# Spatial projection: the features' parts are stored in the first half and fetched in the second, with ten seven-product pairs there instead of six

## The chip, the core and the metric

The kernel runs on one core of a Trainium2 chip. The metric is the device time of one execution in microseconds. Before the change three executions took 2465.49, 2465.73 and 2466.3 us; the median is 2465.73.

## What is computed

A trunk of two layers on 256 positions of width 2048, all in float32. The first layer is a gated MLP with a spatial gate, then a gated MLP with a convolution; the second is latent attention, then the same kind of MLP. After each of the four comes a layer norm. What the change touches is the last product of the first part:

```
z = gelu(x @ w_in);  u, v = split(z, 2);  v = layer_norm(v)
s = einsum('gij,bnjgd->bnigd', masked w_s, v) + b_s
m = (u * s) @ w_out          # (256 x 6144) @ (6144 x 2048): the spatial projection
x = layer_norm(ALPHA * x + m)
```

`u * s` is called the features here.

## The kernel before

**Three products for one.** A float32 operand is split into a high part (a cast to float32r on ACT, ScalarE) and a low part (the value less its high part, a subtraction on DVE, VectorE). A product is made of three matmuls on PE (TensorE): high by high, low by high, high by low (`prod_b`). Weights are split as they are loaded (`Feed._split`, `_cast`, lines 125 and 128): `wh`, `wl`. Features are split in `Acts.make` (lines 487 and 488).

**Units, wide and seven.** The 6144 features are 48 blocks of 128, two blocks to a unit: units 0 to 23. The 2048 output columns are done in two halves of 1024, and each half goes over all 24 units, so each unit is used twice: 0 to 23 in the first half, 23 to 0 in the second. For a unit and a half there are 2 row blocks (positions) x 2 column blocks of 512 x 2 feature blocks, eight products. A **wide** unit (`e` in `PLAN`) makes all eight (`Banks.eight`): 24 matmuls of 512 columns. A **seven** (`s`) makes seven products of sums of blocks instead (`Banks.seven`): 21 matmuls. For that DVE adds up weight blocks (`ts`, line 135), and their sums are split as well (`th`, `tl`), so that such a unit takes five buffers of weights instead of two; and four sums of feature blocks are made (`turn`, lines 291 to 294) and split (lines 483 and 484). The seven-product sums of a half are put together once, after its last seven (`rest`, lines 450 to 454, and `fold`).

**Order and buffers.** `PLAN` is written by hand: for each half the units in order with their kinds. `down` goes through it: for each unit it calls `acts.make` for this unit and the two behind it, takes weights from the feed (split two to three units ahead), and issues the matmuls. Features made in the first half are dropped from `acts.got` and made again in the second half, but for those that are used again very soon (`KEEP`). Loaded weights have three buffers (`raw`), loads go through SP's queue. Split weights and split features share one pool of 14 buffers of 1 MB (`big`). A wide unit's features take half a buffer; two wide units share one, and it is free when both have been used (`self.room`). A seven's features take a buffer. An instruction that writes a buffer waits until the last matmul that reads its former content is done. The last three units of the second half, 2, 1 and 0, are held back (`skew`) and multiplied at the end, one output bank after the other, so that the layer norm can begin on the first bank.

Names in the profile: `wo_q`, `wo_p`, `wo_e` are the output banks of the second half; `wo8sx` is the split features of unit 8 made as a seven, `wo8st` its sums, `wo7wx` a buffer of wide units whose first is 7; `ub` the banks of the first half; `raw` loaded weights; `res` the residual; `lnt` the transposes of the layer norm that follows.

**Stores and fetches that are there already.** In the two later down projections some pairs are "parked": split ahead of time, stored in DRAM through POOL's queue (`kept...`) and fetched through the same queue (`fwh`, `fwl`, `fth`, `ftl`), four transfers of 768 KB to 1 MB one behind the other.

Of the kernel before, what the change touches and what calls it, by code (L numbers as in the profile page):

```python
# [21 lines left out]
NF_GM = HALF // P  # L22
# [32 lines left out]
T1, T2 = 6, 5  # L55
# [4 lines left out]


PLAN = {NF_GM: ("0e 1e 2s 3e 4e 5s 6e 7e 8s 9e 10e 11s 12e 13e 14s 15e 16e 17s 18e 19e 20s 21e 22e 23e",
                "23e 22e 21e 20s 19e 18e 17s 16e 15e 14s 13e 12e 11s 10e 9e 8s 7e 6e 5s 4e 3e 2e 1e 0e"),
        NF_FF: ("0e 1p 2e 3s 4e 5e 6p 7e 8s 9e 10e 11p 12e 13s 14e 15p 16e 17s 18e 19s 20e 21e",
                "21e 20e 19p 18e 17s 16e 15p 14e 13s 12e 11p 10s 9e 8s 7p 6e 5s 4e 3e 2e 1e 0e")}
KINDS = {"e": "wide", "s": "seven", "p": "parked"}
# [143 lines left out]
def trunk(ctx: ExitStack, tc: tile.TileContext, x, xT, gm_in, gm_wout, ffn_up, ffn_dn,  # L210
          ml_q, ml_kv, ml_b, ml_out, consts, w_sT, b_s, ropes, ln_rows, out):
    nc = tc.nc
# [25 lines left out]
    def behind(ins):  # L238

        if recent[0] is not None and feed.used > 0:  # L240
            order(ins, recent[0])
# [46 lines left out]
    def turn(t, k1, k2):  # L288

        at = lambda k, b: k[:, b] if len(k.shape) == 3 else k[:, b * P : (b + 1) * P]  # L290
        tc.keep_in_program_order(nc.vector.tensor_tensor(t[:, 0], at(k1, 0), at(k1, 1), ALU.subtract))
        nc.vector.tensor_tensor(t[:, 1], at(k1, 1), at(k2, 1), ALU.subtract)
        nc.vector.tensor_tensor(t[:, 2], t[:, 1], at(k1, 0), ALU.subtract)
        nc.vector.tensor_tensor(t[:, 3], at(k2, 0), t[:, 2], ALU.add)
# [11 lines left out]
    for j in range(4):  # L306
        t = slot([P, 4, S], f"xraw{j}", tag="side")
# [97 lines left out]
    class Banks:  # L405


        def __init__(self, tag, names, tiles=None):
            self.tag, self.begun = tag, set()
            self.acc = dict(zip(names, tiles)) if tiles else {n: bank(f"{tag}_{n}") for n in names}  # L410
# [45 lines left out]

    class Acts:

        def __init__(self, src, tag, n_k):
            self.src, self.tag, self.n_k = src, tag, n_k  # L460
            self.got, self.room = {}, None

        def make(self, u, kind, tag="big"):

            if u in self.got and (kind == "wide" or self.got[u][1]):
                return
            name, n = f"{self.tag}{u}{kind[0]}", min(2, self.n_k - 2 * u)
            x = self.src[u // 4][:, 2 * u % 8 : 2 * u % 8 + n]
            if kind == "wide":
                if self.room is None:  # L470
                    self.room = slot([P, 4, 512], f"{name}x", F32R, tag)
                    t = self.room[:, 0:n]
                else:
                    t, self.room = self.room[:, 2 : 2 + n], None
                hi, lo = t[:, :, 0:S], t[:, :, S : 2 * S]
                sums = None
            else:
                r = slot([P, 2, 8 * P], f"{name}x", F32R, tag)
                flat = [r[:, h].rearrange("p (s c) -> p s c", s=8) for h in range(2)]
                hi, lo = [r[:, h, 0 : 4 * P].rearrange("p (k c) -> p k c", k=2) for h in range(2)]  # L480
                t = tp.tile([P, 4, P], F32, tag="t2", name=f"{name}t", bufs=T2)
                turn(t, x[:, 0], x[:, 1])
                nc.scalar.copy(flat[0][:, 4:8], t)
                tc.keep_in_program_order(nc.vector.tensor_tensor(flat[1][:, 4:8], t, flat[0][:, 4:8].bitcast(F32), ALU.subtract))
                sums = [(flat[0][:, 4 + i], flat[1][:, 4 + i]) for i in (1, 2, 0, 3)]
            by = (lambda t: t.rearrange("p n (b c) -> p n b c", b=2)) if len(x.shape) == 4 else lambda t: t
            nc.scalar.copy(by(hi), x)
            tc.keep_in_program_order(nc.vector.tensor_tensor(by(lo), x, by(hi).bitcast(F32), ALU.subtract))
            parts = [[(hi[:, j, b * P : (b + 1) * P], lo[:, j, b * P : (b + 1) * P]) for j in range(n)]
                     for b in range(2)]  # L490
            self.got[u] = (parts, sums)
# [108 lines left out]
    class Norm:  # L600
# [150 lines left out]
    for gi in range(6):  # L751
# [3 lines left out]
        for c, p in enumerate(V_PAIRS[gi]):  # L755
# [29 lines left out]
        for i, (n, t) in enumerate(zip(DIRECT, rest)):  # L785
            o = vt[:, i // 2, (i % 2) * 512 : (i % 2) * 512 + 512]
# [48 lines left out]
        norm_v(0, f, rows)  # L835

    pT = [t.rearrange("p b (f c) -> p f b c", c=P) for t in v]
    acts = Acts(pT, "wo", NF_GM)
    def spatial(g, tiles):

        for i, t in enumerate(tiles):
# [25 lines left out]
    for g in range(6):  # L867
# [26 lines left out]
        for i, t in enumerate(rest):  # L894
            o = v[g][:, i // 2, i % 2 * 512 : i % 2 * 512 + 512]
# [133 lines left out]
    for c in range(6):  # L1029
        hi, lo = feed.next()  # L1030
# [321 lines left out]
```

## Time and profile before

| what | value |
|---|---|
| median of three timed executions | 2465.73 us |
| span of the profiled execution | 2464.6 us |
| PE busy | 2458.1 us, 12494 matmuls |
| DVE busy | 2054.7 us |
| ACT busy | 1459.3 us |
| POOL busy | 104.2 us |
| spatial projection, second half, first to last of its banks' regular units | 662.4 to 772.8 us |
| moved by DMA | 611.94 MB, 248 GB/s on average |

The profile is of one execution, taken apart from the timed ones; the span runs from its first to its last instruction, and no time of that execution other than the span is given. Timeline rows hold the start in us, the duration in us, the engine and line, the operation and its tiles, how many follow each other, and in brackets the idle time before and what ended it. Durations overlap the next instruction by a little, so costs are read from start to start. Matmuls overlap too: a pair of 0.61 us and one of 0.39 are 0.68 us from start to start.

### The profile page before, as it was taken

The numbers are of one execution on the slowest core, as the hardware profiler recorded it, in microseconds if no ns is written. First come the engines' busy times: TensorE is split into PE (matmuls) and PEld (weight loads), VectorE is DVE, ScalarE is ACT, GpSimd is POOL, SyncE is SP. The second block draws the span as 40 slices with busy tenths as digits, with TensorE's granted clock in tenths as the row PEclk, the third lists the DMA queues.
The fourth block names the chain that finished last, engine by engine and source line by source line (L and its number), as shares of the span: only waits on it lengthen the run. The fifth ranks groups of instructions, "written<-read, shape, count | busy, mean of one in ns | idle before, by whom it ended". The sixth has DMA issues, their size and how long they took to land. (4 is left out here: it accounts for less than half of the span.)

```text
span 2464.6 us, 32483 instructions
## 1 busy us (share of the span) xinstructions
PE 2458.1 (100%) x12494; PEld 2091.3 (85%) x12494; DVE 2054.7 (83%) x2734; ACT 1459.3 (59%) x1967; POOL 104.2 (4%) x202
## 2 busy tenths in 40 slices
PE   9999999999999999999999999999999999999999
PEld 7888888888888888888888888988888888888887
DVE  7999999989897788778777997867598787878798
ACT  6666665566565666656554566665565665555453
POOL 0000000000000000000001000000000000000000
PEclk9999999999999999999999999999999999999999
DMA  7555666656665778778868885544478787777885
GB/s 291 202 208 205 226 204 202 205 188 205 222 212 198 241 282 314 300 279 300 322 218 318 301 301 182 184 170 156 172 269 309 275 305 304 295 265 278 299 324 201
DMA packets 116428, 611.94 MB, mean 248 GB/s; under 512 B 10648, under 2 KB 10912, under 8 KB 75184
## 3 DMA queue, kind: packets, MB, share of 16 engines
q1 hardware_dynamic: 90128, 462.47, 52.9%
q0 software_dynamic: 26144, 147.39, 15.8%
q8 instruction: 98, 1.61, 0.3%
q14 instruction: 58, 0.48, 0.1%
HBM read 544.75 MB, written 65.06 MB: 247 GB/s over the span
## 5 line engine op out<-in xcount | busy, mean ns | idle before, releaser
L128 DVE TENSOR_TENSOR wl<-raw,wh 128x1024 fp32r<-128x1024 f32 (+4 forms) x645 | 958.4, 1501 | 169.5 <-ACT wh L125 124.0
L125 ACT CAST wh<-raw 128x1024 fp32r<-128x1024 f32 (+4 forms) x645 | 809.0, 1278 | 356.8 <-PE up L230 80.7
L230 PE MATMUL up<-xhl,wh 128*128 128x512 f32 x2624 | 611.4, 390 | 0.0
L230 PEld LDWEIGHTS up<-xhl,wh 128*128 128x128 f32 x2624 | 487.4, 188 | 97.8
L230 PEld LDWEIGHTS up<-xhl,wl 128*128 128x128 f32 x2624 | 325.8, 192 | 6.4
L230 PE MATMUL up<-xhl,wl 128*128 128x256 f32 x2624 | 328.1, 283 | 0.0
L125 ACT CAST th<-ts 128x1536 fp32r<-128x1536 f32 (+1 forms) x138 | 142.5, 1052 | 110.9 <-DVE ts L135 80.3
L230 PE MATMUL ub<-wh,xhl 128*128 128x512 f32 x576 | 179.5, 393 | 0.0
L128 DVE TENSOR_TENSOR tl<-ts,th 128x1536 fp32r<-128x1536 f32 (+1 forms) x138 | 163.2, 1221 | 10.4 <-PE dn_p L230 3.4
L230 PEld LDWEIGHTS ub<-wh,xhl 128*128 128x128 f32 x576 | 108.1, 188 | 24.2 <-issue 1.9
L230 PE MATMUL ub<-wl,xhl 128*128 128x512 f32 x288 | 112.1, 389 | 0.0
L135 DVE TENSOR_TENSOR ts<-ts,raw 128x512 f32<-128x512 f32 x138 | 95.1, 689 | 1.4
L135 DVE TENSOR_TENSOR ts<-raw 128x1024 f32<-128x1024 f32 x69 | 84.3, 1221 | 6.1 <-PE ub L230 3.8
L230 PE MATMUL mo<-wh,oT 128*128 128x512 f32 x256 | 82.5, 401 | 0.0
L230 PE MATMUL v_q<-wh,xhl 128*128 128x512 f32 x224 | 70.7, 391 | 0.3 <-ACT wh L125 0.3
L230 PEld LDWEIGHTS ub<-wl,xhl 128*128 128x128 f32 x288 | 54.1, 188 | 11.3
L230 PE MATMUL v_p<-wh,xhl 128*128 128x512 f32 x192 | 59.9, 389 | 0.0
L230 PEld LDWEIGHTS mo<-wh,oT 128*128 128x128 f32 x256 | 45.5, 189 | 7.1
L230 PEld LDWEIGHTS v_q<-wh,xhl 128*128 128x128 f32 x224 | 42.0, 188 | 10.5 <-ACT wh L125 1.9
L230 PE MATMUL mo<-wl,oT 128*128 128x512 f32 x128 | 50.1, 391 | 0.0
L724 ACT ACTIVATE lny<-lnt,lncol 128x128 f32<-128x128 f32 x96 | 36.6, 472 | 15.6 <-PE lnt L720 15.5
L388 DVE TENSOR_TENSOR h_0a<-up,lo_0a 128x256 f32<-128x256 f32 x41 | 17.2, 421 | 33.0 <-ACT lo_0a L386 33.0
(1838 smaller groups left out, 4338.4 us busy)
## 6 DMA issues: line engine op xcount, KB each, us to landing
raw<-in_ffn_up_dram SPq DMA_DIRECT2D x172, 1024.0 KB, 7.0
raw<-in_gm_in_dram SPq DMA_DIRECT2D x93, 1024.0 KB, 5.3
raw<-in_ffn_dn_dram SPq DMA_DIRECT2D x68, 1024.0 KB, 7.2
raw<-in_gm_wout_dram SPq DMA_DIRECT2D x48, 1024.0 KB, 5.3
praw<-in_ffn_dn_dram POOLq DMA_DIRECT2D x16, 1024.0 KB, 13.9
keptth<-pth POOLq DMA_DIRECT2D x16, 1024.0 KB, 8.1
kepttl<-ptl POOLq DMA_DIRECT2D x16, 1024.0 KB, 8.8
fth<-keptth POOLq DMA_DIRECT2D x16, 1024.0 KB, 9.4
```

The source lines that it names most:

```text
L125: cast = self.nc.scalar.copy(hi, raw)
L128: self.nc.vector.tensor_tensor(lo, raw, hi.bitcast(F32), ALU.subtract)
L135: add = lambda o, a, b: self.nc.vector.tensor_tensor(o, a, b, ALU.add)
L230: recent[0] = nc.tensor.matmul(o, l, r, start=start, stop=stop, skip_group_check=True)
L388: nc.vector.tensor_tensor(h, acc[:, 0:S], lo, ALU.add)
L724: nc.scalar.activation(y[:, j], t[:, j * P : (j + 1) * P], AF.Identity, bias=lncol[:, o : o + 1], scale=lncol[:, g : g + 1])
```

## The change

In the first half each unit from 3 to 21 has its split features stored in DRAM right after they are made (`keep`). In the second half `make` looks whether a unit was stored. If it was stored in the kind now wanted, the whole buffer is fetched and nothing is computed. If it was stored wide and is wanted as a seven (16, 13, 10 and 7), its high and low parts are fetched in two transfers and only the sums are made and split. Units 23, 22, 2, 1 and 0 are as before. In the second half's line of `PLAN` four more units become sevens: 16, 13, 10 and 7. Stores and fetches all go through POOL's queue.

```diff
-                "23e 22e 21e 20s 19e 18e 17s 16e 15e 14s 13e 12e 11s 10e 9e 8s 7e 6e 5s 4e 3e 2e 1e 0e"),
+                "23e 22e 21e 20s 19e 18e 17s 16s 15e 14s 13s 12e 11s 10s 9e 8s 7s 6e 5s 4e 3e 2e 1e 0e"),
...
+        def keep(self, u, kind, t):
+
+            if u not in self.store or u in self.away:
+                return
+            d = dram.tile(list(t.shape), F32R, tag=f"{self.tag}{u}away", name=f"{self.tag}{u}away", bufs=1)
+            tc.keep_in_program_order(nc.gpsimd.dma_start(d, t))
+            self.away[u] = (kind, d)
+
+        def fetch(self, o, d):
+
+            ins = tc.keep_in_program_order(nc.gpsimd.dma_start(o, d))
+            behind(ins)
...
+            was, d = self.away.get(u, (None, None))
...
+                if was == kind:
+                    self.fetch(t, d)
...
+                if was == kind:
+                    self.fetch(r, d)
+                else:
+                    if was:
+                        for o, c in ((hi, slice(0, S)), (lo, slice(S, 2 * S))):
+                            self.fetch(o, d[:, :, c])
+                    t = tp.tile([P, 4, P], F32, tag="t2", name=f"{name}t", bufs=T2)
+                    turn(t, x[:, 0], x[:, 1])
+                    nc.scalar.copy(flat[0][:, 4:8], t)
...
-            nc.scalar.copy(by(hi), x)
-            tc.keep_in_program_order(nc.vector.tensor_tensor(by(lo), x, by(hi).bitcast(F32), ALU.subtract))
+            if was is None:
+                nc.scalar.copy(by(hi), x)
+                tc.keep_in_program_order(nc.vector.tensor_tensor(by(lo), x, by(hi).bitcast(F32), ALU.subtract))
+                self.keep(u, kind, t if kind == "wide" else r)
...
-    acts = Acts(pT, "wo", NF_GM)
+    acts = Acts(pT, "wo", NF_GM, [u for u in range(3, 22)])
```

How this moves the instructions is seen at three places of the second half. The first is DVE, from the end of unit 14's weights on. Before, with unit 13 wide: `wo13wx` are the parts of its features and of unit 12's, the two rows `wl` of 2048 columns the weights of 13 and 12, `wo11st` and `wo8st` sums of features, `ts_5283` unit 11.

```order
L128 TENSOR_TENSOR tl_5175<-ts_5171,th_5174 128x1536
L128 TENSOR_TENSOR tl_5175<-ts_5171,th_5174 128x512
L488 TENSOR_TENSOR wo13wx<-v_1373,wo13wx 128x2x256
L128 TENSOR_TENSOR wl_5215<-raw_5138,wh_5214 128x2048
L488 TENSOR_TENSOR wo13wx<-v_1373,wo13wx 128x2x256
L128 TENSOR_TENSOR wl_5247<-raw_5185,wh_5246 128x2048
L291 TENSOR_TENSOR wo11st<-v_1070 128x128
L292 TENSOR_TENSOR wo8st<-v_1070 128x128
L293 TENSOR_TENSOR wo8st<-wo8st,v_1070 128x128
L294 TENSOR_TENSOR wo8st<-v_1070,wo8st 128x128
L135 TENSOR_TENSOR ts_5283<-raw_5218 128x1024
L484 TENSOR_TENSOR wo11sx<-wo11st,wo11sx 128x512
```

The same stretch of DVE after the change, with unit 13 a seven (`ts_5246`, `wl_5248`, `tl_5250`), down to unit 12's weights (`wl_5288`):

```order
L128 TENSOR_TENSOR tl_5203<-ts_5199,th_5202 128x1536
L128 TENSOR_TENSOR tl_5203<-ts_5199,th_5202 128x512
L291 TENSOR_TENSOR wo13st<-v_1373 128x128
L135 TENSOR_TENSOR ts_5246<-raw_5174 128x1024
L292 TENSOR_TENSOR wo10st<-v_1070 128x128
L135 TENSOR_TENSOR ts_5246<-ts_5246,raw_5174 128x512
L128 TENSOR_TENSOR wl_5248<-raw_5174,wh_5247 128x1536
L507 TENSOR_TENSOR wo13sx<-wo13st,wo13sx 128x512
L135 TENSOR_TENSOR ts_5246<-ts_5246,raw_5174 128x512
L128 TENSOR_TENSOR tl_5250<-ts_5246,th_5249 128x1536
L128 TENSOR_TENSOR tl_5250<-ts_5246,th_5249 128x512
L128 TENSOR_TENSOR wl_5288<-raw_5213,wh_5287 128x2048
```

Where one subtraction of 2048 columns stood for unit 13 stand six steps and the split of its sums; the two feature parts of 13 and 12 are gone, and so is unit 11's split of its own sums and features.

The second place is POOL's queue. Before, the last rows of the gate's normalization (`vr`) are followed by the next stage's parked pairs:

```order
L808 DMA vr_3433<-gbrows 128x512
L808 DMA vr_3506<-gbrows 128x512
L808 DMA vr_3508<-gbrows 128x512
L162 DMA praw_6409<-in_ffn_dn_dram 128x2x1024
L629 DMA resd_0_6940<-res_0_4608 128x2048
```

After, 19 stores and then 23 fetches stand between them; these are the last stores and the fetches down to unit 13 (`x2`: high and low part apart):

```order
L469 DMA wo20away<-wo20sx 128x2048
L469 DMA wo21away<-wo21wx 128x1024
L474 DMA wo23wx<-wo21away 128x1024
L474 DMA wo20sx<-wo20away 128x2048
L474 DMA wo19wx<-wo19away 128x1024
L474 DMA wo19wx<-wo18away 128x1024
L474 DMA wo17sx<-wo17away 128x2048
L474 DMA wo16sx<-wo16away 128x2x256 x2
L474 DMA wo15wx<-wo15away 128x1024
L474 DMA wo14sx<-wo14away 128x2048
L474 DMA wo13sx<-wo13away 128x2x256 x2
L474 DMA wo15wx<-wo12away 128x1024
```

The wide units of a shared buffer are now 21 with 23, 19 with 18, 15 with 12, 9 with 6, and 4 with 3; the store of each unit is ahead of every fetch in the queue.

The third place is the end of the half on DVE, from the weights of unit 2 (`wl_5590` before, `wl_5629` after) to the features of unit 0. Before:

```order
L128 TENSOR_TENSOR wl_5586<-raw_5524,wh_5585 128x2048
L128 TENSOR_TENSOR wl_5590<-raw_5557,wh_5589 128x2048
L658 SCALAR_TENSOR_TENSOR res_1_5507<-res_1_5507,wo1p_5618 128x512
L451 TENSOR_TENSOR wo1u_5619<-wo_p_4900,wo1p_5618 128x512
L452 TENSOR_TENSOR wo1w<-wo_q_4898,wo1u_5619 128x512
```

After:

```order
L128 TENSOR_TENSOR wl_5625<-raw_5568,wh_5624 128x2048
L683 SCALAR_TENSOR_TENSOR res_1_5551<-res_1_5551,wo1p_5657 128x512
L451 TENSOR_TENSOR wo1u_5658<-wo_p_4938,wo1p_5657 128x512
L128 TENSOR_TENSOR wl_5629<-raw_5597,wh_5628 128x2048
L452 TENSOR_TENSOR wo1w<-wo_q_4936,wo1u_5658 128x512
```

Unit 2's weights have moved behind the first two steps that fold the seven-product sums; all steps of the end are still there.

More of the change, by code (lines that the diff above doesn't have):

```diff
@@ L457, in trunk, with __init__ @@
     class Acts:
-        def __init__(self, src, tag, n_k):
+        def __init__(self, src, tag, n_k, store=()):
             self.src, self.tag, self.n_k = src, tag, n_k
             self.got, self.room = {}, None
+            self.store, self.away = store, {}
+        def keep(self, u, kind, t):
[7 more added lines that the diff above has]
+            behind(ins)
         def make(self, u, kind, tag="big"):
@@ L480, in make @@
                 hi, lo = [r[:, h, 0 : 4 * P].rearrange("p (k c) -> p k c", k=2) for h in range(2)]
[L481 to L484, printed above, removed]
+                if was == kind:
[7 more added lines that the diff above has]
+                    nc.scalar.copy(flat[0][:, 4:8], t)
+                    tc.keep_in_program_order(nc.vector.tensor_tensor(flat[1][:, 4:8], t, flat[0][:, 4:8].bitcast(F32), ALU.subtract))
                 sums = [(flat[0][:, 4 + i], flat[1][:, 4 + i]) for i in (1, 2, 0, 3)]
             by = (lambda t: t.rearrange("p n (b c) -> p n b c", b=2)) if len(x.shape) == 4 else lambda t: t
-            nc.scalar.copy(by(hi), x)
-            tc.keep_in_program_order(nc.vector.tensor_tensor(by(lo), x, by(hi).bitcast(F32), ALU.subtract))
+            if was is None:
+                nc.scalar.copy(by(hi), x)
+                tc.keep_in_program_order(nc.vector.tensor_tensor(by(lo), x, by(hi).bitcast(F32), ALU.subtract))
+                self.keep(u, kind, t if kind == "wide" else r)
             parts = [[(hi[:, j, b * P : (b + 1) * P], lo[:, j, b * P : (b + 1) * P]) for j in range(n)]
```

## The prediction

> **What bounds the kernel now.** I read the table of engines first, then the list of what TensorE (PE) waited for, then the stage that the change touches, stretch by stretch.
>
> ```profile
> PE 2458.1 (100%) x12494; PEld 2091.3 (85%) x12494; DVE 2054.7 (83%) x2734; ACT 1459.3 (59%) x1967; POOL 104.2 (4%) x202
> ```
>
> ```profile
> PE warm L230 <- POOL idle L281: 1.3, 1, 1.3
> PE fin L230 <- DVE dg L701: 0.3, 1, 0.3
> PE v_q L230 <- ACT wh L125: 0.3, 1, 0.3
> ```
>
> The first row is the page's, the other three are the whole answer on PE's waits. They are every wait of PE that the trace names: 1.9 us in all, at the start, in the first projection and at the very end. None lies in the spatial projection. So in this stage time is won only by giving PE fewer matmuls, and lost only by making PE wait where it doesn't now.
>
> The stretches below hold five times three units of the second half, 17 to 3, of 15.64 us each; the sum row is over all five. The columns are PE, weight loads, DVE (VectorE), ACT, POOL, granted clock, DMA share and GB/s.
>
> ```profile
> 694.57:710.21 15.64, 15.64 (x71) 12.95 (x70) 15.04 (x20) 9.40 (x9) 0.00 (x0) 1.00 0.66 233
> ...
> sum 78.20, PE 78.20 PEld 64.75 DVE 69.61 ACT 47.51 POOL 0.00; mean PE 15.64 PEld 12.95 DVE 13.92 ACT 9.50 POOL 0.00
> ```
>
> PE is full at clock 1.00. DVE has 69.6 of 78.2 us: it is the engine that can become late. ACT has a third to spare.
>
> **The matmuls removed.** From the timeline of PE, the first matmul of unit 8 (a seven), of unit 7 (wide), of the unit after, and of unit 0 among the held-back ones:
>
> ```profile
> 741.49 0.61 PE L230 MATMUL wo_q<-wh,wo8sx 128*128 128x512 f32 x2
> ...
> 746.25 0.61 PE L230 MATMUL wo_q<-wh,wo7wx 128*128 128x512 f32 x2
> ...
> 751.69 0.61 PE L230 MATMUL wo_q<-wh,wo7wx 128*128 128x512 f32 x2
> ...
> 775.49 0.61 PE L230 MATMUL wo_q<-wh,wo0wx 128*128 128x512 f32 x2
> ```
>
> (The row at 751.69 still says wo7wx because units 7 and 6 share a buffer.) A seven takes 746.25 - 741.49 = 4.76 us for 21 matmuls, a wide unit 751.69 - 746.25 = 5.44 us for 24: 0.227 us each either way. Units 16, 13, 10 and 7 become sevens: 4 x 0.68 = **2.72 us** less on PE, on the path that sets the end. That is the most the change can give, since no PE wait is there to be removed. It is 0.11%; a measurement of this kernel can tell about 0.2%, 4.9 us, from no change.
>
> **What DVE gets instead.** The timeline of DVE through one round of the half: the four small sums of a seven's features, the pair sums ts, the feature parts, the weight parts wl and tl.
>
> ```profile
> 724.58 0.29 DVE L291 TENSOR_TENSOR wo8st<-v 128x128 f32<-128x128 f32 x1
> ...
> 726.05 1.23 DVE L135 TENSOR_TENSOR ts<-raw 128x1024 f32<-128x1024 f32 x1 [0.33 <-PE wo_q L230]
> 727.19 0.68 DVE L484 TENSOR_TENSOR wo8sx<-wo8st,wo8sx 128x512 fp32r<-128x512 f32 x1
> 727.79 0.68 DVE L488 TENSOR_TENSOR wo8sx<-v,wo8sx 128x512 fp32r<-128x512 f32 x1
> 728.39 0.68 DVE L135 TENSOR_TENSOR ts<-ts,raw 128x512 f32<-128x512 f32 x1
> 729.00 1.75 DVE L128 TENSOR_TENSOR wl<-raw,wh 128x1536 fp32r<-128x1536 f32 x1
> 730.66 0.68 DVE L135 TENSOR_TENSOR ts<-ts,raw 128x512 f32<-128x512 f32 x1
> 731.27 2.35 DVE L128 TENSOR_TENSOR tl<-ts,th 128x1536 fp32r<-128x1536 f32 x2
> 733.54 0.68 DVE L488 TENSOR_TENSOR wo7wx<-v,wo7wx 128x512 fp32r<-128x512 f32 x1
> 734.14 2.28 DVE L128 TENSOR_TENSOR wl<-raw,wh 128x2048 fp32r<-128x2048 f32 x1
> 736.34 0.68 DVE L488 TENSOR_TENSOR wo7wx<-v,wo7wx 128x512 fp32r<-128x512 f32 x1
> ```
>
> Start to start, a seven's weights cost 1.14 + 0.61 + 1.66 + 0.61 + 2.27 = 6.29 us, a wide unit's 2.20, a feature part 0.60, four small sums 726.05 - 0.33 - 724.58 = 1.14. Per round of three units: before, one seven, two wide, four feature parts, four sums: 6.29 + 4.40 + 2.40 + 1.14 = 14.2 us against 15.64 of PE. After, two sevens, one wide, and for the unit that was stored wide the sums and one part: 12.58 + 2.20 + 1.14 + 0.60 = **16.5 us against 14.96**. So in the four rounds 16-5 DVE falls back 1.5 us a round; the parts not remade (9 wide units, 6 sevens, the wide part of four more) don't make up for four more sevens. DVE must live on its lead, and the lead is capped by the 14 buffers of the pool.
>
> In the built order, the last weight part of unit 16 (tl) takes a buffer that unit 18's last matmul frees, so it can't start before PE reaches unit 17, at 694.57 in this trace. From there DVE has to do, up to the low part of unit 0: that tl 2.27, seven more sevens 44.0, nine wide units 19.8, sums and part of 13, 10 and 7 5.2, the eight steps that fold the seven-product sums, and three feature parts 1.8. The fold and the end of the line, with the two idles left after the last seven:
>
> ```profile
> 752.13 2.29 DVE L128 TENSOR_TENSOR wl<-raw,wh 128x2048 fp32r<-128x2048 f32 x1 [1.38 <-ACT wh L125]
> ...
> 757.16 4.49 DVE L128 TENSOR_TENSOR wl<-raw,wh 128x2048 fp32r<-128x2048 f32 x2 [2.13 <-issue]
> 761.57 0.69 DVE L658 SCALAR_TENSOR_TENSOR res<-res,wo1p 128x512 f32<-128x512 f32 x1
> ...
> 766.50 0.68 DVE L488 TENSOR_TENSOR wo2wx<-v,wo2wx 128x512 fp32r<-128x512 f32 x1
> ...
> 772.11 0.68 DVE L488 TENSOR_TENSOR wo0wx<-v,wo0wx 128x512 fp32r<-128x512 f32 x1
> ```
>
> The fold is 766.50 - 761.57 = 4.9 us. Sum 78.0: DVE ends this at 694.57 + 78.0 = 772.6 if it never idles. PE wants it at 775.49 - 2.72 = 772.8. Today it is ready at 772.79 for a use at 775.49, with 2.7 us of cover; afterwards the cover is 0.2 us, and each idle of DVE goes straight to PE at unit 0. Bounds: no idle, a stall of 0; both idles above remain (3.5 us), 3.3. The 2.13 came from buffers that PE freed, and PE now comes earlier while DVE comes later, so I take 1.0 us of idle: a stall of **0.8 us**. Ahead of it the cover never goes below zero by the same sums; it is thinnest at unit 7, whose tl ends about 1.5 us before its first use.
>
> **The transfers.** Stored: 13 wide units of 512 KB and 6 sevens of 1 MB, 12.5 MB; fetched: 9 x 0.5 + 6 x 1 + 4 x 0.5 MB, the same. All go through POOL's queue, which in this stage has nothing else; behind them stands the first load of the next stage's parked pairs, which is made only in the up projection. The nearest rows are weight loads and the later stages' stores and fetches (KB each, median us to landing):
>
> ```profile
> raw<-in_ffn_dn_dram SPq DMA_DIRECT2D x68, 1024.0 KB, 7.2
> raw<-in_gm_wout_dram SPq DMA_DIRECT2D x48, 1024.0 KB, 5.3
> ...
> keptth<-pth POOLq DMA_DIRECT2D x16, 1024.0 KB, 8.1
> ...
> ftl<-kepttl POOLq DMA_DIRECT2D x16, 1024.0 KB, 11.9
> ```
>
> For fth, the issue on POOL in ns and the spread of landing:
>
> ```profile
> L187 POOL DMA_DIRECT2D fth<-keptth x16: 528/531/563, 1207.4 to 2394.8; - x16
> ...
> DMA to landing us min/median/max: 7.2/9.4/21.4
> ```
>
> For fwh, 768 KB and first of its four in the queue, between 1300 and 1385 us:
>
> ```profile
> DMA to landing us min/median/max: 5.7/7.0/9.4
> ```
>
> A 1 MB fetch for a seven takes a buffer that is free after nine matmuls of the seven three units ahead: 2.72 + 4.76 + 5.44 = 12.9 us of room. fth, 9.4, fits; ftl's 11.9 has 2.5 MB before it in its queue, which a fetch here hasn't. The fetches of 15 and 9 wait for the last matmul of 18 and 12 and have two sevens, 9.5 us, 4's has 10.2: at 512 KB, by fwh's 7.0 for 768 KB, they fit with 2.5 us left. Cost 0. The weight loads get slower, 5.3 to about 7.2 us, but one is issued as soon as the weights three units back are read, and DVE then has at least 2.27 + 6.29 + 2.20 = 10.8 us of other work: 0. In the first half only stores are added: a part is written two units (4.76 + 5.44 = 10.2 us) or more before PE has read it and its buffer can be taken again, against 8.1 for a 1 MB store: 0.
>
> A round now moves three weight loads and 2 MB of features, 5 x 1.05 = 5.24 million bytes in 14.96 us: 350 GB/s, where the first round above has 233. The mean rates in 40 slices of the span, and what the chip carried in a later stage while PE was full:
>
> ```profile
> GB/s 291 202 208 205 226 204 202 205 188 205 222 212 198 241 282 314 300 279 300 322 218 318 301 301 182 184 170 156 172 269 309 275 305 304 295 265 278 299 324 201
> ```
>
> ```profile
> 1310.00:1320.00 10.00, 10.00 (x46) 8.26 (x44) 6.39 (x9) 5.31 (x6) 0.00 (x0) 1.00 1.06 418
> 1320.00:1330.00 10.00, 10.00 (x46) 8.28 (x45) 9.20 (x13) 4.38 (x5) 0.00 (x0) 1.00 0.69 255
> 1330.00:1340.00 10.00, 10.00 (x46) 8.29 (x45) 3.99 (x4) 4.43 (x6) 2.11 (x4) 1.00 0.97 342
> 1340.00:1350.00 10.00, 10.00 (x46) 8.29 (x45) 9.93 (x16) 5.10 (x6) 0.00 (x0) 1.00 1.03 403
> ```
>
> The mean of the four is 354 with bursts to 418, and no wait of PE. So 350 is carried, with a sixth to spare. [...]
>
> **Sum.** -2.72 + 0.8 = -1.9 us. The profiled execution spans 2464.6 us, 1.1 under the median of the three timed runs, 2465.73; the saving is the same in both. Forecast **2463.8 us**, its own range 2463.0 to 2465.2.
>
> **Rivals.**
> The tail eats the gain. DVE keeps idles of 3 us or more after the last seven and unit 0 is late by the whole 2.7: **2465.7**. For it: the two idles above, and 78.2 - 69.6 = 8.6 us in which DVE isn't busy in the five rounds; against: an idle that ends on a buffer from PE shrinks when DVE's lead does.
> Late fetches, the slower side. The features of 15, 9 and 4 come after PE is there. This decides from 9.5 us of landing. At ftl's 11.9 PE waits 2.4 + 2.4 + 1.7 = 6.5 us, DVE catches up meanwhile, and the time is 2465.7 - 2.7 + 6.5 = **2469.5**; it passes the 0.2% at 12.3 us, or by one fetch at fth's 21.4. For it: 350 GB/s over 60 us, where no slice above has over 324. Against: fwh never took over 9.4 in the stretch shown, and these are smaller.
> POOL held up by DVE. If a descriptor write on POOL had to wait for the running DVE instruction, each fetch would land up to 2.3 us later (the longest step), 9.3 for fwh's 7.0 and 11.7 for fth's 9.4: just in time. With two such waits in a fetch, 11.6 and 14.0: 2.1 + 2.1 + 1.4 us at 15, 9 and 4, and 1.1 at each of the sevens 14, 11, 8 and 5, 10 us together: **2473**. Against: fth's issue took 528 to 563 ns in all 16 cases. [...]
> That the change doesn't do what it says: "not remade" is not quite so, since 16, 13, 10 and 7 remake their sums; this is in the sum above.
>
> **Chances.** Forecast 0.69; tail 0.14; late fetches 0.14, half of it over 4.9 us; POOL 0.02; something faster that no row shows 0.01. Faster by over 0.2%: 0.01; within: 0.69 + 0.14 + 0.07 = 0.90; slower: 0.07 + 0.02 = 0.09. The range goes from the full gain less the 0.4 us by which the runs differ, 2462.6, to 2467.6, which takes in the tail and the first part of the late fetches.
>
> **What would show it.** PE 12 matmuls fewer; the first normalization transposes 1.5 to 2.7 us earlier than now; PE's waits naming DVE wo0wx with 0.3 to 1.5 us; DVE's waits in units 16 to 5 nearly gone; fetches of 512 KB at 6 to 7.5 us, 1 MB at 8 to 10; some 350 GB/s from 695 to 755 us. Waits of PE on a fetch, or on wl or tl of units 13 to 5, would prove the working wrong.

## The result and the profile after

The changed kernel takes 2470.92 us (median of 14 runs, 2468.97 to 2472.63); the kernel before, run beside it, 2465.61 us (14 runs, 2464.89 to 2466.3). The ratio is 1.0022 with a 95% interval of 1.0014 to 1.0029: 5.3 us slower. The forecast was 2463.8 us, in a range up to 2467.6. The profiled execution of the changed kernel spans 2469.1 us, that of before 2464.6.

The table of engines of the changed kernel. PE has its 12 matmuls less:

```profile
PE 2457.8 (100%) x12482; PEld 2090.9 (85%) x12482; DVE 2055.4 (83%) x2725; ACT 1454.8 (59%) x1954; POOL 127.9 (5%) x244
```

All of PE's waits in the changed kernel (who waited for whom: us in total, times, longest). Three of the rows are new, and all three lie in the last units of the half:

```profile
PE wo_q L230 <- DVE wo2wx L512: 3.7, 1, 3.7
PE warm L230 <- POOL idle L281: 1.3, 1, 1.3
PE wo_q L230 <- DVE wo0wx L512: 0.7, 1, 0.7
PE fin L230 <- DVE dg L726: 0.3, 1, 0.3
PE wo_q L230 <- DVE wl L128: 0.2, 1, 0.2
```

The timeline of PE in the changed kernel: first matmul of unit 2 (the first of the held-back units), the next one, first of unit 0, the next one, and the first transposes of the layer norm behind the half:

```profile
770.47 0.39 PE L230 MATMUL wo_q<-wh,wo2wx 128*128 128x512 f32 x1
774.60 0.56 PE L230 MATMUL wo_q<-wh,wo2wx 128*128 128x512 f32 x1 [3.74 <-DVE wo2wx L512]
...
779.08 0.39 PE L230 MATMUL wo_q<-wh,wo0wx 128*128 128x512 f32 x1
780.21 0.50 PE L230 MATMUL wo_q<-wh,wo0wx 128*128 128x512 f32 x1 [0.74 <-DVE wo0wx L512]
...
790.14 0.60 PE L745 MATMUL lnt<-ident,res 128*128 128x128 f32 x4
```

The same two points in the kernel before:

```profile
772.77 0.61 PE L230 MATMUL wo_q<-wh,wo2wx 128*128 128x512 f32 x2
...
785.24 0.60 PE L720 MATMUL lnt<-ident,res 128*128 128x128 f32 x4
```

Up to unit 2 the change does what it should: PE is there at 770.47, 2.30 us sooner than before. Then all of it is lost and more: the transposes come 4.90 us later than before. From 770.47 to 774.60 one matmul of 0.23 us was made, so 3.90 us are lost; from 779.08 to 780.21 another 0.90. Between these two, 11 matmuls take 779.08 - 774.60 = 4.48 us where 11 x 0.227 = 2.50 would do: 1.98 us. The windows of the changed kernel show PE's clock there, and the stages before it (columns as in the prediction; the clock is the first of the last three):

```profile
700.00:720.00 20.00, 20.00 (x90) 16.58 (x89) 19.97 (x24) 11.98 (x11) 3.90 (x6) 1.00 0.96 341
720.00:740.00 20.00, 20.00 (x90) 16.57 (x89) 19.93 (x23) 11.87 (x11) 3.03 (x5) 1.00 1.00 334
740.00:755.00 15.00, 15.00 (x68) 12.40 (x67) 14.49 (x14) 9.23 (x7) 2.31 (x4) 1.00 0.97 338
755.00:765.00 10.00, 10.00 (x45) 8.07 (x43) 4.05 (x2) 2.39 (x2) 0.00 (x0) 1.00 1.02 404
...
774.00:776.00 2.00, 1.40 (x4) 1.14 (x5) 2.00 (x2) 1.15 (x2) 0.00 (x0) 0.73 0.25 102
776.00:778.00 2.00, 1.89 (x6) 0.98 (x4) 2.00 (x3) 1.24 (x2) 0.00 (x0) 0.50 0.27 33
```

After the wait the granted clock is 0.73, then 0.50. The sum is -2.30 + 3.90 + 1.98 + 0.90 = +4.5 of the 4.9 us at the transposes; 0.4 us is spread behind them. The 1.98 us are only where PE lost the time: the second matmul of unit 0 starts at 780.21 us because DVE is done with `wo0wx` at 779.47 + 0.69 = 780.16 (row below), so at full clock PE would have waited there instead.

The upper rows tell where it began. From 700 us on the DMA share is 0.96 to 1.02: the DMA engines are full. And from 755 to 765 us, while they move 404 GB/s, DVE works 4.05 us of 10. It waits for ACT, and ACT for weights. ACT in the changed kernel, the casts of the weights of units 4, 3 and 2:

```profile
752.78 1.91 ACT L125 CAST wh<-raw 128x2048 fp32r<-128x2048 f32 x1
761.02 1.91 ACT L125 CAST wh<-raw 128x2048 fp32r<-128x2048 f32 x1 [6.33 <-DMA raw<-in_gm_wout_dram]
...
766.11 1.91 ACT L125 CAST wh<-raw 128x2048 fp32r<-128x2048 f32 x1 [2.70 <-DMA raw<-in_gm_wout_dram]
```

DVE in the changed kernel, the low parts of the same three, the rest of the fold of the sevens (it begins at 765.17 and goes on at 770.26), and the first and the last low part of the features that PE waits for:

```profile
754.73 2.29 DVE L128 TENSOR_TENSOR wl<-raw,wh 128x2048 fp32r<-128x2048 f32 x1 [0.24 <-ACT wh L125]
762.96 2.29 DVE L128 TENSOR_TENSOR wl<-raw,wh 128x2048 fp32r<-128x2048 f32 x1 [5.95 <-ACT wh L125]
...
768.05 2.29 DVE L128 TENSOR_TENSOR wl<-raw,wh 128x2048 fp32r<-128x2048 f32 x1 [1.59 <-ACT wh L125]
770.26 0.68 DVE L452 TENSOR_TENSOR wo1w<-wo_q,wo1u 128x512 f32<-128x512 f32 x1
...
773.86 0.69 DVE L512 TENSOR_TENSOR wo2wx<-v,wo2wx 128x512 fp32r<-128x512 f32 x1
...
779.47 0.69 DVE L512 TENSOR_TENSOR wo0wx<-v,wo0wx 128x512 fp32r<-128x512 f32 x1
```

In these rows the low weights of 2 (768.05) stand ahead of the rest of the fold (770.26), and the fold ahead of `wo2wx` (773.86); so when the weights of unit 2 land late, everything behind them is late by as much. From 768.05 us to the end of `wo0wx` DVE has no idle time left in which it could catch up. The load of unit 2, in the changed kernel (the answer on `raw` for the stretch around 752 us) and in the kernel before (around 748 us):

```profile
L96 SPq DMA_DIRECT2D raw<-in_gm_wout_dram x1: 379/379/379, 752.3 to 752.3; - x1
...
DMA to landing us min/median/max: 13.7/13.7/13.7
```

```profile
L96 SPq DMA_DIRECT2D raw<-in_gm_wout_dram x1: 378/378/378, 747.6 to 747.6; - x1
...
DMA to landing us min/median/max: 5.5/5.5/5.5
```

It is issued 4.7 us later and takes 8.2 us longer: the weights of 2 land at 766.0 instead of 753.1 us. The issue is late because it waits for DVE to be done with the buffer, the weights three units back (DVE's last sum of them ends at 751.54 + 0.68 = 752.22 us, the issue comes at 752.3), and DVE is behind with four more sevens. What is under way beside it, from SP's and POOL's timelines of the changed kernel: the residual's second half, the loads of 3 to 0, the fetch of 3, and the first load of the next stage's parked pairs.

```profile
744.08 0.81 SPq L644 DMA_DIRECT2D res<-in_x_dram  x2
748.11 17.54 SPq L96 DMA_DIRECT2D raw<-in_gm_wout_dram  x4
```

```profile
749.62 0.54 POOL L474 DMA_DIRECT2D wo4wx<-wo3away  x1
750.14 0.73 POOL L162 DMA_DIRECT2D praw<-in_ffn_dn_dram  x1
```

That last load stood elsewhere before. POOL in the kernel before:

```profile
668.59 0.72 POOL L162 DMA_DIRECT2D praw<-in_ffn_dn_dram  x1 [222.85 <-DVE wo20sx L488]
```

It was made as soon as a buffer was free, at 668.6 us, where the DMA share is 0.57 in the 20 us around it. Now the stores and fetches of 19 units stand ahead of it on POOL, the last of them at 749.62 us, and it goes at 750.14, into the fullest stretch.

### The profile page after: what moved, and what is told of

Read it like the earlier page. It is cut to its first block, busy times and chain, and to the rows that moved or that the text cites. A ratio compares the mean times of both kernels' runs of the same rounds, so it can differ in the third digit from the quotient of the medians.

```text
span 2469.1 us, 32569 instructions
## 1 busy us (share of the span) xinstructions
PE 2457.8 (100%) x12482; PEld 2090.9 (85%) x12482; DVE 2055.4 (83%) x2725; ACT 1454.8 (59%) x1954; POOL 127.9 (5%) x244
## 5 line engine op out<-in xcount | busy, mean ns | idle before, releaser
L125 ACT CAST th<-ts 128x1536 fp32r<-128x1536 f32 (+1 forms) x146 | 150.9, 1051 | 128.9 <-DVE ts L135 104.0
L128 DVE TENSOR_TENSOR tl<-ts,th 128x1536 fp32r<-128x1536 f32 (+1 forms) x146 | 172.7, 1222 | 11.4 <-ACT th L125 3.4
L135 DVE TENSOR_TENSOR ts<-ts,raw 128x512 f32<-128x512 f32 x146 | 100.7, 690 | 1.5
```

What stands on the lines that cost most here:

```text
L125: cast = self.nc.scalar.copy(hi, raw)
L128: self.nc.vector.tensor_tensor(lo, raw, hi.bitcast(F32), ALU.subtract)
L135: add = lambda o, a, b: self.nc.vector.tensor_tensor(o, a, b, ALU.add)
```

## The experiments

The theory after this reading (theory 1): the weights of 3 and 2 land late because of the transfers that are moved at the end of the half; PE then runs into DVE's chain. Its rival (theory 2): ten sevens are too much for DVE, so the tail is late whatever the transfers do. A third: all the added traffic slows everything a little. The runs of before beside these kernels had medians of 2465.6 to 2465.9 us. A table at the end of this section sets the kernels side by side.

**Each half of the change alone.** The changed kernel with the six sevens of before:

```diff
-   "23e 22e 21e 20s 19e 18e 17s 16s 15e 14s 13s 12e 11s 10s 9e 8s 7s 6e 5s 4e 3e 2e 1e 0e"),
+   "23e 22e 21e 20s 19e 18e 17s 16e 15e 14s 13e 12e 11s 10e 9e 8s 7e 6e 5s 4e 3e 2e 1e 0e"),
```

> The changed kernel with the six sevens of before: features stored and fetched, no matmul saved. Theory 1 (a burst of transfers at the end of the half delays the weight load of unit 3, so that DVE gets the weights of 2 and 0 late): the burst is the same, so PE still waits 2 to 4 us at units 2 and 0; before is 2465.6, so 2467.5 to 2470. Theory 2 (four more sevens are too much for DVE at the tail, whatever the transfers do): DVE has less work than before, so no wait at the tail, 2465.6 within 0.5. Theory 3 (the sum of all the added traffic slows everything a little): 2466 to 2468, with small waits outside the tail.

2466.14 us, ratio 1.0003 (0.9994 to 1.0012): no difference. Theory 1's 2467.5 to 2470 is missed; the time lies at the edges of what theories 2 and 3 gave. But its trace shows slow loads all the same: unit 2's takes 12.8 us, and ACT waits 4.9 us for it. PE doesn't wait at the tail, for two reasons. With six sevens DVE is less behind, so this load is issued at 747.0 us instead of 752.3 and its weights land at 759.8 instead of 766.0. And PE comes to unit 2 1.8 us later, at 772.25. So the traffic alone takes away the cover and costs nothing yet.

And the ten sevens with nothing stored:

```diff
-    acts = Acts(pT, "wo", NF_GM, [u for u in range(3, 22)])
+    acts = Acts(pT, "wo", NF_GM)
```

> The changed kernel with nothing stored: ten sevens, all features remade. A round of three units costs DVE 12.58 + 2.20 + five feature parts 3.0 + two times four sums 2.28 = 20.1 us against 14.96 of PE, 5.1 us too much in each of four rounds, less a lead of some 8 to 12 us. All theories expect waits of PE on weights in units 13 to 5 and at the tail: 2471 to 2478. If it came out at 2463 to 2465 the transfers alone would be the loss and the sevens would need no fetches.

2479.17 us (5 runs), ratio 1.0055 (1.0042 to 1.0068), a little over what was expected. Two of PE's waits in this kernel, on weights that ACT doesn't get done; they lie in the sevens of units 10 and 7:

```profile
PE wo_q L230 <- ACT wh L125: 2.3, 2, 2.0
PE wo_q L230 <- ACT th L125: 2.0, 2, 1.0
```

The four more sevens need the fetches: those are worth 2479.2 - 2470.9 = 8.3 us to them.

**The first parked load moved out of the way.** First ahead, between the fetches of 19 and 18:

```diff
+                if hf == 1 and i == 2 and tag == "wo":
+                    feed.load_early(parked[0])
...
-        raw = tile("praw", F32)
-        pin(nc.gpsimd.dma_start(raw.rearrange("p (k c) -> p k c", k=ap.shape[1]), ap))
+        raw = self.early.pop(i, None)
+        if raw is None:
+            raw = tile("praw", F32)
+            pin(nc.gpsimd.dma_start(raw.rearrange("p (k c) -> p k c", k=ap.shape[1]), ap))
```

> The changed kernel, but the first parked pair's load (praw, 1 MB) stands in POOL's queue behind the fetch of unit 19 instead of behind that of unit 3, so it goes at about 670 to 690 us as before. Theory 1 with praw as the last straw of the burst: unit 3's weights land in time, the waits at 2 and 0 fall from 4.4 to under 1.5 us, PE's clock there stays at 1.00: 2463.5 to 2466. Theory 2 (DVE): as the changed kernel, 2470.9 within 0.7. Theory 3 (all the traffic): half of the loss at most goes, 2468.5 to 2470.5.

Then behind, through SP's queue in its place of the up projection:

```diff
-        pin(nc.gpsimd.dma_start(raw.rearrange("p (k c) -> p k c", k=ap.shape[1]), ap))
+        load = nc.sync if len(self.kept) == 1 else nc.gpsimd
+        pin(load.dma_start(raw.rearrange("p (k c) -> p k c", k=ap.shape[1]), ap))
```

> The changed kernel, but the first parked pair's load goes through SP's queue in its place of the up projection, some 100 us after the tail. Theory 1: as with the early load, waits at 2 and 0 under 1.5 us, 2463.5 to 2466. Theory 2: 2470.9 within 0.7. Theory 3: 2468.5 to 2470.5. Should the early load help and the late one not, it is not the burst but something the first parked pair itself needs.

2469.24 us, ratio 1.0013 (1.0005 to 1.0022), and 2469.18 us, ratio 1.0014 (1.0005 to 1.0023). Both ways the same 1.7 us, so it is the place among the transfers and not anything that the parked pair needs. But it is only a third of the loss: theory 1's 2463.5 to 2466 is missed, theory 2's 2470.2 to 2471.6 as well, and the 2468.5 to 2470.5 of the third theory holds both. The waits with the load ahead:

```profile
PE wo_q L239 <- DVE wo2wx L521: 3.2, 2, 2.1
...
PE wo_q L239 <- DVE wo0wx L521: 1.2, 1, 1.2
```

They still sum to 4.4 us, at a clock of 1.00. The weights of 2 are there 2.9 us sooner, and DVE begins their low part 2.05 us sooner, at 766.00 instead of 768.05, now held up by the weights of 3 alone. The transposes come 2.06 us sooner, so it is DVE's start and not the clock that was won.

**The residual earlier.**

```diff
-                if i == n - 8:
+                if i == (n - 13 if hf and tag == "wo" else n - 8):
                     ln.fetch(hf)
```

> The changed kernel, but the second half of the residual (two loads of 512 KB on SP's queue) is loaded five units earlier, at unit 12 instead of 7; it holds one of the 14 buffers that much longer. Theory 1 (the load of unit 3's weights lands late because of the transfers beside it): one of the four MB beside it goes, it lands some 2 us sooner, 2468 to 2469.5. Theory 2 (DVE has too much to do, the transfers don't matter): 2470.9 within 0.7. If the buffer is missed instead, new waits at units 10 to 8 and 2472 or more.

2468.39 us, ratio 1.0011 (1.0003 to 1.002), as theory 1 had it: 2.5 us gained, and no new wait in the units 12 to 8.

**Two fetches less at the end.**

```diff
-    acts = Acts(pT, "wo", NF_GM, [u for u in range(3, 22)])
+    acts = Acts(pT, "wo", NF_GM, [u for u in range(5, 22)])
```

> The changed kernel, but units 4 and 3 are not stored and fetched but remade, as before: 1 MB less beside the load of unit 3's weights, two more feature parts (1.2 us) on DVE. Theory 1: 2468.5 to 2470. Theory 2: 2471 to 2472.5, by the 1.2 us more on DVE. Together with the first parked pair's load, which was worth 1.7 us, and the early residual, the sum says whether the burst alone explains the loss.

2470.45 us, ratio 1.002 (1.0011 to 1.0029): between the two theories and no different from the changed kernel. The weights of 2 land 1.4 us sooner, but the remade parts of 4 and 3 add to ACT and DVE, and PE waits 1.6 us for the low weights of unit 3. This run doesn't tell the theories apart.

**Nine sevens.** Unit 7 is wide again, which gives DVE 4 us:

```diff
-   "... 9e 8s 7s 6e 5s 4e 3e 2e 1e 0e"),
+   "... 9e 8s 7e 6e 5s 4e 3e 2e 1e 0e"),
```

> The changed kernel with unit 7 wide again: nine sevens, so DVE is 4 us less behind when it comes to the weights of 6, 5 and 4, and 0.68 us more on PE. All transfers as in the changed kernel but for unit 7's, one of 512 KB for two of 256. A theory in which the burst alone is to blame: unit 3's weights land as late as now and PE still waits 2 us or more, 2468 to 2470. A theory in which it takes both, DVE so late that the buffer for unit 3's load comes free only at 748 us, and the burst behind it: the load goes 4 us sooner, no wait, 2465.8 - 2.0 + 0.3 = 2464.1, 2463.5 to 2465.5.

2469.56 us, ratio 1.0014 (1.0005 to 1.0023), in the range of the theory that blames the transfers alone. The form that takes a late DVE as well, with the load 4 us sooner and no wait left, missed. PE's waits:

```profile
PE wo_q L230 <- DVE wo3wx L512: 3.3, 1, 3.3
...
PE wo_q L230 <- DVE wo1wx L512: 0.8, 1, 0.8
```

(Units 3 and 2 share a buffer here.) The loads of 3 and 2 are issued 2.5 us sooner, at 745.6 and 749.8, and that of 2 still takes 13.8 us. So its weights land 2.4 us sooner, and by the medians the kernel is 1.4 us faster than the change although PE has three matmuls more. Less work for DVE does help, through the earlier issue, about as much as one moved transfer; it doesn't shorten the load.

**Two spare buffers for weights.** Same work, same transfers, but the loads of 5 to 0 stand one step further ahead, in a chain of four to five buffers instead of three:

```diff
-        t = self.pool.tile([P, 2048], F32, tag="raw", name=f"raw{self.loaded}", bufs=SLOTS["raw"])
+        tag = "side" if self.loaded in self.spare else "raw"
+        t = self.pool.tile([P, 2048], F32, tag=tag, name=f"raw{self.loaded}", bufs=SLOTS[tag])
...
+    feed.spare = [n_gm - 1 - u for u in (6, 3)]
```

> The changed kernel with ten sevens, but the weights of units 6 and 3 are loaded into two buffers of the other pool that are free by then, so that the loads of 5 to 0 no longer wait for DVE to be done with the weights three units back. Same transfers, same work of DVE. Theory 1 in the form that needs both (late buffer, then burst): unit 3's load goes at 745 us or sooner, DVE's wait of 6 us goes, PE's waits at 2 and 0 fall under 1 us: 2463.5 to 2466. Theory 2 (too much work on DVE): the waits at 2 and 0 stay over 2 us, 2468 to 2471. Theory 3 (all the traffic): 2468 or more.

2467.49 us, ratio 1.0007 (0.9998 to 1.0016): 3.4 us gained without an operation less on DVE, so theory 2 in its plain form (2468 to 2471) is out. Theory 1's 2463.5 to 2466 is missed too, and the waits are not all under 1 us:

```profile
PE wo_q L231 <- DVE wo2wx L515: 1.9, 2, 1.1
...
PE wo_q L231 <- DVE wo0wx L515: 1.1, 1, 1.1
```

The load of 2 is issued at 744.5 instead of 752.3 us, 7.8 us sooner, but takes 16.6 instead of 13.7: its weights land only 4.9 us sooner.

**The three edits together** (parked load late, residual early, spare buffers), which asks whether DVE's chain is too long by itself:

> The changed kernel with three of the edits together: first parked pair's load late, residual early, two spare buffers for the weights of 6 and 3. Work on DVE and PE unchanged, 2 MB fewer at the end of the half. Theory of the transfers (what is late is when the weights of 3, 2 and 1 land, and that is set by the MB that are moved by then): the weights of unit 2 land by 758 us instead of 766, DVE's fold can begin right after the last seven, no wait over 0.5 us at 2, 1 and 0: the full saving, 2463.0 to 2464.5 against 2465.8 before. Theory of DVE (its chain of wl, fold and parts behind the last seven is too long whatever lands when): waits of 1.1 us each at 2, 1 and 0 stay as in the runs with one edit, 2466 to 2468.

2465.23 us, ratio 1.0 (0.9991 to 1.0009), short of the 2463.0 to 2464.5 that the theory of the transfers gave. Unit 2's weights land at 755.9, and every wait at 2, 1 and 0 is gone, so DVE's chain is not too long by itself. In their place stand two on fetches:

```profile
PE wo_p L232 <- DMA wo7sx<-wo7away: 0.8, 1, 0.8
PE wo_q L232 <- DMA wo8sx<-wo8away: 0.6, 1, 0.6
```

Something that was pulled forward now delays these: the residual, or the weight loads of the spare buffers. The last experiment separates the two.

**1 MB more.** The second parked pair's load put behind the fetch of 3 as well:

```diff
+                if hf == 1 and i == 19 and tag == "wo":
+                    feed.load_early(parked[1])
```

> The changed kernel with 1 MB more on the suspected place: the load of the second parked pair stands right behind the fetch of unit 3 as well, ahead of the first one's, some 100 us before it is needed. Theory of the transfers: at 410 GB/s 1 MB is 2.6 us, so the weights of 2 and 1 land about 2 us later and PE waits about 2 us longer: 2472 to 2475. Theory of DVE: 2470.9 within 0.7.

2471.2 us, ratio 1.0024 (1.0014 to 1.0033), 0.3 us more than the changed kernel: theory 1's 2472 to 2475 is missed, and theory 2's 2470.2 to 2471.6 holds it. In the one profiled execution, itself 0.8 us over the median, unit 2's weights land 1.2 us later and the span is 1.1 us longer: the direction, but not the size. The two parked loads land 16.0 and 20.4 us after their issue, the last at 771.5 us. So a part of the extra MB was moved after unit 2's weights had landed, at 767.2 us. It weakens a simple count of MB; that it matters which bytes go ahead of unit 2's is a reading that no run tests by itself.

**The three edits and no fetches of 4 and 3.**

> The three edits together and in addition units 4 and 3 not stored but remade: another 1 MB less at the end, 1.2 us more on DVE. Theory of the transfers: nothing is left to gain if the three edits suffice, 2463 to 2464.5; if they don't, 1 to 2 us faster than those. Theory of DVE: 1 us slower than the three edits.

2465.17 us, ratio 1.0 (0.9991 to 1.0009), the same as with the three edits: nothing more to gain at the tail. The 2463 to 2464.5 expected for that case is missed, as PE's one wait of the half, 1.6 us on the fetch of unit 7, is still there. Theory 2's 1 us more did not come.

**The residual out of the full stretch altogether**, at unit 21 and into a buffer of the other pool, with the late parked load and the spare buffers:

```diff
-                if i == n - 8:
+                if i == (2 if hf and tag == "wo" else n - 8):
                     ln.fetch(hf)
...
-            t = slot([P, 2, 1024], f"res{self.idx}_{h}")
+            t = slot([P, 2, 1024], f"res{self.idx}_{h}", tag="side" if self.idx == 0 and h else "big")
```

> As the run with the three edits together, but the residual's second half is loaded at unit 21, where the DMA share is 0.65, into a free buffer of the other pool, instead of at unit 12 in one of the 14. No MB of it stands among the transfers from 690 us on. Theory of the transfers: the waits of 0.6 and 0.8 us on the fetches of 8 and 7, which the three edits together brought in, go (their 1 MB less in 720 to 745 us is 2.6 us), and the tail stays clear: the full saving, 2462.5 to 2464 against 2465.6 before, a span of 2461.8 to 2462.3. If those waits come from the weight loads that the spare buffers draw forward instead, they stay, and it is 2464.5 to 2465.5 again.

2463.24 us (11 runs, 2462.21 to 2464.2) against 2465.77 for before beside it: ratio 0.999 (0.9981 to 0.9999). It is 2.5 us faster than before, the fastest of all, and as expected. PE's waits, all of them, and the first transposes:

```profile
PE warm L232 <- POOL idle L285: 1.3, 1, 1.3
PE fin L232 <- DVE dg L730: 0.3, 1, 0.3
```

```profile
782.49 0.60 PE L749 MATMUL lnt<-ident,res 128*128 128x128 f32 x4
```

785.24 - 782.49 = 2.75 us sooner than before: the whole saving of the ten sevens, with all the stores and fetches in place. So the third theory is out: the added traffic as such costs nothing. And with the spare buffers still there, the waits on the fetches of 8 and 7 went with the residual. Moved alone, to unit 12, it had made no such wait, so they took both, the residual there and the loads drawn forward. Whether the three moves would bring anything to the kernel before was not tried; PE has no wait there that they could remove.

**The kernels in one table.** For each: when the load of unit 2's weights was issued, how long it took, when ACT cast them, when DVE began their low part, and the first transposes (all in us, from one profiled execution each), and the median of the timed runs. Kernels in the order of the fourth column. The kernel before and each half of the change alone are not in it, nor are the two in which 4 and 3 are not stored, since the layer norm's first steps come in another order in them.

| kernel | issued | took | cast | low part | transposes | median |
|---|---|---|---|---|---|---|
| residual to unit 21, late parked load, spare buffers | 742.7 | 14.5 | 757.24 | 759.19 | 782.49 | 2463.24 |
| three edits together | 742.6 | 13.3 | 758.25 | 760.20 | 783.87 | 2465.23 |
| spare buffers | 744.5 | 16.6 | 761.19 | 763.14 | 786.37 | 2467.49 |
| residual early | 752.7 | 9.7 | 762.52 | 764.46 | 787.70 | 2468.39 |
| first parked load ahead | 752.2 | 10.9 | 763.17 | 766.00 | 788.08 | 2469.24 |
| first parked load behind | 752.2 | 11.0 | 763.34 | 766.15 | 788.20 | 2469.18 |
| nine sevens | 749.8 | 13.8 | 763.63 | 765.58 | 788.59 | 2469.56 |
| the change | 752.3 | 13.7 | 766.11 | 768.05 | 790.14 | 2470.92 |
| 1 MB more | 752.5 | 14.7 | 767.35 | 769.29 | 791.34 | 2471.20 |

In the seven kernels from the third row on PE waits at the tail, and the transposes come at a fixed distance from the start of DVE's low part of unit 2, whichever edit moved it: 22.05 to 22.09 us in the four (the change, 1 MB more, first parked load ahead and behind) in which two steps of the fold stand ahead of it, 23.0 to 23.2 in the three in which all eight stand behind. In the first two rows PE doesn't wait there any more. That is the finding: at the tail the time is set by when the weights of units 3 and 2 are there, and by DVE's chain behind them. Both the issue (held back by the three buffers: 752.3, with the spare buffers 744.5) and the way (held up by the other MB: 13.7 us, with the residual early 9.7) count, and no single edit is enough. Theory 2 is right in two things: with ten sevens DVE is later to free the buffers, so the load of unit 2 is issued at 752.3 us, where it is 749.8 with nine and 747.0 with six; and DVE's chain has no slack left to swallow a late landing.

## Why the prediction was wrong, point by point

- **The matmuls removed, -2.72 us.** Right in size and place: the first transposes came 2.75 us sooner once nothing else was late.
- **The transfers: "The weight loads get slower, 5.3 to about 7.2 us, but one is issued as soon as the weights three units back are read, and DVE then has at least 2.27 + 6.29 + 2.20 = 10.8 us of other work: 0."** This is the step that failed. The median of the changed kernel's loads, both halves together:

```profile
raw<-in_gm_wout_dram SPq DMA_DIRECT2D x48, 1024.0 KB, 8.1
```

  Through the rounds of sevens, at 5.9 to 9.2 us (the ten loads from 693.6 to 743.4 us), the step held: PE never waited there. At the end of the half it took 12.9 (unit 3), 13.7 and 11.3 us, more than the 10.8 of work, and after the last seven DVE hasn't got that work at all. So the term put at 0 was 5.95 + 1.59 us of DVE's idle time, and DVE was done with unit 0's features at 780.16 us. The prediction's sum had 772.6 if DVE never idles, and 772.6 + 7.5 is 780.1; in the fastest kernel, where the loads are in time, DVE was done at 772.49. One cost was taken for all the loads, from another stage; the end of this one has other transfers (the residual, the parked load) and less cover.
- **"350 is carried, with a sixth to spare."** Carried nearly, at 334 to 341 GB/s and without a wait of PE until the end, but with nothing to spare. Those four windows were a mean share of 0.94 over 40 us with gaps between; here the share stays at 0.96 to 1.02 for 65 us, with 404 GB/s only at the end. The rate alone doesn't tell how long one load takes, nor whether PE waits: the fastest kernel moved 406 GB/s from 740 to 755 us, its load of unit 2, issued at 742.7, took 14.5, and PE's waits name nothing in the half.
- **"behind them stands the first load of the next stage's parked pairs, which is made only in the up projection."** Wrong: the row at 668.59 stands in the trace of before. Made in the up projection's code, it was issued there long before that projection; behind the fetches it goes at 750.14, some 81 us later. That was worth 1.7 us of the loss.
- **The residual** was not in the sum. It was there before, and harmless at 4.5 us to landing; in the full stretch it takes 10.4 us, and moving it was worth 2.5 us.
- **The tail's stall, 0.8 us at unit 0.** At unit 0 nearly right, 0.74 us on DVE. But the larger wait, 3.74 us, came at unit 2, where the prediction had cover. And in the fastest kernel, with ten sevens and no late load, there is no stall at all. The sum for DVE assumed idles that end on buffers from PE, and so shrink when DVE is late. The idles that came (5.95 and 1.59 us) end on loads, and don't shrink.
- **The deadlines of the fetches, cost 0.** Right: in the changed kernel PE waits for no fetch. But from unit 17 on those of 512 KB took 3.5 to 11.8 us, those of 1 MB 6.2 to 10.5, a wider spread than the 6 to 7.5 and 8 to 10 forecast, and they had less room than thought: two were late by 0.6 and 0.8 us as soon as other loads were pulled forward.
- **DVE's waits in units 16 to 5 nearly gone.** Right: 19.97 and 19.93 of 20 us busy from 700 to 740 us.
- **The rivals.** "Late fetches", 2469.5, came near the time by a transfer that is late, but by the wrong one: the weights, not the features. "POOL held up by DVE" did not show: the fetches in one piece took 527 to 543 ns to issue, against 528 to 563 ns for the fetches of before, while DVE was busy up to 19.97 of 20 us; those in two pieces took 703 to 715 ns a piece.

## What to carry to other kernels

A transfer put on a queue can push back what stands behind it there: here the first parked load went from 668.59 to 750.14 us, behind 19 stores and 23 fetches. So look up in the trace when each instruction behind it is issued now, not where the code makes it. Read the DMA share, not the GB/s alone: here 341 GB/s went with a share of 0.96 and 404 with 1.02, and loads that took 5.3 us before took up to 9.2 in the stage and up to 13.7 at its end. The first to be missed was the one whose cover ended, at the end of the stage. And a saving on PE counts only to the next point where it meets something that PE doesn't set: here the 2.30 us won up to 770.47 were lost in the 3.74 us of waiting there. With the residual and the parked load moved out of the full stretch, and two buffers more, the saving was there, 2.75 us at the transposes.

## What the runs showed of the hardware that was not expected

In some of these kernels the granted clock of TensorE was lower for a while after waits of PE, in others it stayed at 1.00, and the longest single wait didn't tell which. In the changed kernel PE waits 3.74 us, up to 774.60. In windows of 0.1 us the clock is 1.00 from 774.8 to 774.9 us, 0.53 in the next; it is 0.50 from 778.2 to 778.3 and 0.90 in the next.

With units 4 and 3 not stored PE waits 2.41 us, up to 774.37, and the clock (the first of the last three numbers) falls:

```profile
774.00:776.00 2.00, 1.63 (x4) 1.34 (x5) 2.00 (x2) 0.36 (x2) 0.00 (x0) 0.50 0.11 45
776.00:778.00 2.00, 2.00 (x7) 1.21 (x6) 2.00 (x3) 1.96 (x2) 0.00 (x0) 0.65 0.40 57
```

With the first parked load ahead it waits 2.10 us, up to 772.54, two waits of 1.14 and 1.17 follow, and the clock stays:

```profile
772.00:774.00 2.00, 1.46 (x6) 1.05 (x6) 2.00 (x2) 1.63 (x3) 0.00 (x0) 1.00 0.19 78
774.00:776.00 2.00, 0.86 (x4) 0.57 (x4) 2.00 (x3) 1.32 (x2) 0.00 (x0) 1.00 0.25 33
```

With nothing stored, the longest wait near unit 7 is 2.00 us, a second of 0.97 follows (in the 20 us below PE is busy for all but 2.97), and the mean clock is 0.83:

```profile
740.00:760.00 20.00, 17.03 (x62) 13.13 (x61) 19.31 (x27) 11.47 (x12) 0.00 (x0) 0.83 0.52 170
```

So a longest wait of 2.10 us came without a lower clock and one of 2.00 us with it; what decides it these runs don't show. In the changed kernel the low clock cost PE 1.98 us but the kernel nothing: the distance from DVE's low part of unit 2 to the transposes is 22.09 us with it and 22.08 without it (first parked load ahead).
